# Accumulating transfers for some low weight parts, five more Strassen-like units, and another order of shared additions in a split-precision encoder trunk

## The chip, the cores and the metric

One core of a Trainium2 chip. The metric is device time in microseconds (us) from the first to the last instruction of one execution and what lies around it; a run's number is the time of that one core, and the number given for a kernel is the median of its runs.

## The reference, cut to what matters

256 tokens of width D = 2048 pass two layers (a 2-D neighbourhood attention, then a short gated convolution). Each mixer is followed by a gated MLP with a width-3 convolution and D_FF = 5632. All is float32.

```python
def conv_glu_ffn(x, w_up, conv_w, conv_b, w_down):
    h = dwconv_centered(x @ w_up, conv_w) + conv_b
    g, u = jnp.split(h, 2, axis=-1)
    return (jax.nn.silu(g) * u) @ w_down

for i in range(DEPTH):                      # DEPTH = 2
    a = rms_norm(h, mix_norm[i])
    mixed = neighborhood_attention(...) if i == 0 else short_conv_mixer(...)
    h = h + mixed                           # both end in "@ w_o" / "@ w_out", 2048 x 2048
    h = h + conv_glu_ffn(rms_norm(h, ffn_norm[i]), ...)
return rms_norm(h, final_norm)
```

The change is in the products that return to the width of 2048: attention's output (`wo`), the short convolution's output (`wscout`) and the MLP's down projection (`wdown`), which each add to `h`.

## The kernel before

**Split products.** A float32 operand is written as a high part `hi` (rounded to the type that TensorE takes at full rate) and a low part `lo` = value minus `hi`. `product` (L355 to L359) makes a product from three matmuls into one PSUM bank: L357 activation-high x weight-high, L358 activation-high x weight-low, L359 activation-low x weight-high.

**Weights.** A chunk of 512 KB (128 x 1024) is loaded on SP's queue into a buffer `raw` (L109 in row layout, L113 in the column layout of the groups below). `parts` (L119) then splits it: ScalarE casts it to `hi` (L128), VectorE subtracts to make `lo` (L129). There are 5 `raw`, 6 `hi` and 6 `lo` buffers, and `prep_to` (L101) runs four chunks (AHEAD) ahead of TensorE. A chunk's `raw` comes free when its last reader is done, and SP's next load waits for that.

**Phases** (`Phase`, L144) do the up projections, qkv and the input of the short convolution; TensorE's rows of it are L174 and L182. **Groups** (`Tokens`, L292) do the projections that return to 2048 columns. An MLP is done in two halves of 22 tiles of 128 hidden channels; after each half a `Tokens` adds its share to `h`. A `Tokens` has two column groups g = 0, 1 of 1024 columns; four PSUM banks ("mm": 11, 21, 12, 22, two token halves by two column halves) collect a group's sums. The group's depth goes by units of two tiles, unit i being tiles 2i and 2i+1, and each unit has a left and a right chunk.

- A *normal* unit does eight products (24 matmuls of 128x512): the left chunk's four, then the right chunk's four.
- A unit in the set `sset` is a *seven* (L361): seven products of combined operands. Its right chunk goes through `sums` (L132), four VectorE additions of 128x512 (L138 to L141) that make two combined weight tiles, one of them in another `raw` buffer; three splits follow (a half-size w22, and t13 and t24). The combined activations ("forms") come from `make_forms` (L396): four POOL operations and a split of 128x512. Four products go to banks of their own, a, e, f, b ("mu", in the buffers that other stages use under the tags st, sc, tr, o), which stay open from the group's first seven to its last. In the order in which they run, the seven products write a, 11, 12, e, f, b, 21.

At a group's end four residual additions (L262, VectorE) add the mm banks to `h` and so free them for the next group. After the last seven, `combine` (L380) copies a (L384, ScalarE) and adds e, f, b to `h` with eight VectorE operations; the line `after(due, ...)` in `seven` queues it for so many ticks later, a tick being one item of TensorE's work, so `due` says behind which residuals and low parts it stands.

**Plans.** For each `Tokens` a table gives, per group, the units' order, the sevens and `due`: `S_FIRST` for the first half of an MLP, `S_SECOND` for the second, `S_ATT` for attention's output, `S_OUT` for the short convolution's. Groups start in the profile at 308.4 us (`wo`), 644.7, 1003.8, 1390.6 (`wscout`), 1723.1 and 2082.1 and end 57 to 118 us later.

The order on each engine is the program's own order after a scheduling layer has moved instructions; each engine runs its queue in order and waits for semaphores.

Of the kernel before, what the change touches and what calls it, by code (L numbers as in the profile page):

```python
# [16 lines left out]
F32R = mybir.dt.float32r  # L17
AF = mybir.ActivationFunctionType
ALU = mybir.AluOpType
# [3 lines left out]
P = 128  # L23
D = 2048
S = 256
KT = D // P
# [8 lines left out]
CH = 8  # L35
# [4 lines left out]

ORDER = tuple(range(HALF // 2))
S_FIRST = ((ORDER, (1, 3, 5, 7, 9), 3), (ORDER, (3, 5, 7, 9), 6))

S_SECOND = (((0, 2, 1, 4, 3, 6, 5, 8, 7, 9, 10), (1, 3, 5, 7), 1), (ORDER, (3, 5, 7), 1))
S_OUT = (1, 3, 5)
S_ATT = (((0, 1, 2, 6, 3, 7, 4, 5), (6, 7), 1),) * 2


C_NORM = 0
# [9 lines left out]
def trunk(ctx, tc, xT, par, bias, wqk, wv, wo, wsc, wscout, wup, wdown, out):  # L61
    nc = tc.nc
# [41 lines left out]
    def prep_to(n):  # L104
        while len(prepped) < min(n, len(chunks)):
            src, w, kind = chunks[len(prepped)]
            raw = wp.tile([P, CH * P], F32, name="raw", tag="raw", bufs=5)
            if kind == "rows":
                nc.sync.dma_start(out=raw[:, :w], in_=src)  # L109
                prepped.append(parts(raw[:, :w]) + (raw,))  # L110
                continue

            nc.sync.dma_start(out=raw.rearrange("p (f c) -> p f c", f=4), in_=src.rearrange("f p c -> p f c"))  # L113
            r = raw.rearrange("p (f k c) -> p f k c", f=4, c=P)
            if kind == "cols":
                prepped.append(parts(r) + (raw,))
            else:
                prepped.append(sums(prepped[-1][2].rearrange("p (f k c) -> p f k c", f=4, c=P), r))

    def parts(r):  # L120

        hi = wp.tile([P, CH * P], F32R, name="hi", tag="hi", bufs=6)
        lo = wp.tile([P, CH * P], F32R, name="lo", tag="lo", bufs=6)
        if len(r.shape) == 4:
            hv, lv = (x[:, :4 * r.shape[2] * P].rearrange("p (k f c) -> p f k c", f=4, c=P) for x in (hi, lo))
        else:
            hv, lv = (x[:, :r.shape[1]] for x in (hi, lo))
        nc.scalar.copy(out=hv, in_=r)  # L128
        nc.vector.tensor_sub(out=lv, in0=r, in1=hv.bitcast(F32))  # L129
        return hi, lo  # L130

    def sums(l, r):  # L132

# [158 lines left out]
    class Tokens:  # L292
# [4 lines left out]
        def __init__(self, w, nk, src, evac, plan, forms, halves=0):  # L297


            self.src, self.evac, self.plan, self.forms, self.nk = src, evac, plan, forms, nk  # L300
            self.halves = halves
            for g, (order, sset, _) in enumerate(plan):
                for i in order:
                    k = 2 * i
                    left, right = (w[f:f + 4, :, k * P:(k + 2) * P] for f in (8 * g, 8 * g + 4))
                    c = len(chunks)
                    if g == KT // 8 - 1 and k >= nk - halves:
                        if k == nk - halves:
                            items.append((self, g, c, k, k, nk))
                            ends.append(c + halves)  # L310
                        chunks.extend(((left, 8 * P, "cols"), (right, 8 * P, "cols")))
                        continue
                    chunks.append((left, 8 * P, "cols"))
                    if i in sset:
                        chunks.append((right, 8 * P, "sums"))
                        items.append((self, g, c + 1, k, k, k + 2))
                        ends.append(c + 2)
                    else:
                        chunks.append((right, 8 * P, "cols"))
                        items.append((self, g, c, k, k, k + 2))  # L320
                        items.append((self, g, c + 1, k, k, k + 2))
                        ends.extend((c + 1, c + 2))

        def run(self, g, c, k0, ka, kb):
            order, sset, _ = self.plan[g]
            if kb - ka > 2:
                return self.finale(g, c, ka)
            if k0 // 2 in sset:
                return self.seven(g, c, k0)
            hi, lo, _ = prepped[c]  # L330
            right = len(prepped[c - 1]) == 3 and (self, g, c - 1, k0, ka, kb) in items[item[0] - 1:item[0]]
            first, last = ka == 2 * order[0], kb == 2 * order[-1] + 2
            if first and not right:
                self.c = {n: pm.tile([P, 4 * P], F32, name="mm", tag="mm") for n in ("11", "21", "12", "22")}
            for t in range(2):
                ps = self.c["12"[t] + "12"[right]]
                for k in range(ka, kb):
                    x = self.src[k]
                    wh, wl = (w[:, (k - k0) * 4 * P:(k - k0 + 1) * 4 * P] for w in (hi, lo))
# [20 lines left out]

        def seven(self, g, c, k0):  # L361
            i = k0 // 2
            order, sset, due = self.plan[g]
            s_order = [j for j in order if j in sset]
            first, last = i == s_order[0], i == s_order[-1]
            if first:
                self.u = [pa.tile([P, 4 * P], F32, name="mu", tag=n) for n in ("st", "sc", "tr", "o")]
            a, e, f, b = self.u
            left, (w22, t13, t24) = prepped[c - 1], prepped[c]
            fh, fl = self.forms[i]  # L370
            s1, s2, s4, s3 = ((fh[:, j * P:(j + 1) * P], fl[:, j * P:(j + 1) * P]) for j in range(4))
            raw = lambda k, t: tuple(self.src[k0 + k][:, j + t * P:j + (t + 1) * P] for j in (0, S))
            for ps, x, w, j in ((a, raw(0, 0), left, 0), (self.c["11"], raw(1, 0), left, 1), (self.c["12"], s4, w22, 0),
                                (e, s1, t13, 0), (f, s3, t13, 1), (b, s2, t24, 0), (self.c["21"], raw(1, 1), t24, 1)):
                own = ps in self.u
                self.product(ps, *x, *(y[:, j * 4 * P:(j + 1) * 4 * P] for y in w[:2]), own and first, own and last)
            if last:
                after(0 if self.halves and g == KT // 8 - 1 else due, lambda u=self.u: self.combine(g, *u))

        def combine(self, g, a, e, f, b):  # L380

            sa, u = (tp.tile([P, 4 * P], F32, name="s", tag="s") for _ in range(2))
            o = {(t, n): h[:, t, (2 * g + n) * 4 * P:(2 * g + n + 1) * 4 * P] for t in range(2) for n in range(2)}
            nc.scalar.copy(out=sa, in_=a)  # L384
            nc.vector.tensor_add(out=u, in0=b, in1=sa)
# [328 lines left out]
    Tokens(wscout, KT, yT, to_norm(3, a3), ((range(KT // 2), S_OUT, 1),) * 2, yforms)  # L714
    mlp(1, a3, last_evac())


# [132 lines left out]
```

## Time and profile before

| | |
|---|---|
| median of 3 runs | 2214.65 us (2214.26 to 2214.70) |
| the profiled execution | 2215.03 us, of which the span is 2213.2 us |
| granted TensorE clock, mean | 0.998 |
| TensorE (PE) busy | 2198.8 us, 99% of the span |
| VectorE (DVE), ScalarE (ACT), GpSimd (POOL) busy | 1743.6, 1275.6, 71.5 us |
| DMA engines, mean busy share | 58.2% for SP's weight loads |

In the profile's lines the columns are: busy time, mean nanoseconds of one, and the idle time of the engine just before, with what ended most of it ("<- DVE lo L129": a semaphore from that line). In a timeline the columns are the start and length in us, then engine, line, operation, output and inputs, and in brackets the idle time before. PE's instructions are pipelined: one that takes 0.39 us starts 0.23 us after the last. "DMA to landing" or the third column of the DMA issues is the time from a DMA's issue until its bytes have landed. PEld is TensorE's weight load, which runs beside its matmuls.

### The profile page before, as it was taken

The numbers are of one execution on the slowest core, as the hardware profiler recorded it, in microseconds if no ns is written. First come the engines' busy times: TensorE is split into PE (matmuls) and PEld (weight loads), VectorE is DVE, ScalarE is ACT, GpSimd is POOL, SyncE is SP. The second block draws the span as 40 slices with busy tenths as digits, with TensorE's granted clock in tenths as the row PEclk, the third lists the DMA queues.
The fourth block names the chain that finished last, engine by engine and source line by source line (L and its number), as shares of the span: only waits on it lengthen the run. The fifth ranks groups of instructions, "written<-read, shape, count | busy, mean of one in ns | idle before, by whom it ended". The sixth has DMA issues, their size and how long they took to land.

```text
span 2213.2 us, 31934 instructions
## 1 busy us (share of the span) xinstructions
PE 2198.8 (99%) x11782; PEld 1902.3 (86%) x11782; DVE 1743.6 (79%) x2665; ACT 1275.6 (58%) x1896; POOL 71.5 (3%) x115
## 2 busy tenths in 40 slices
PE   9999999999999999999999999999999999999998
PEld 8888888888888888888888888888888888888886
DVE  8677678877788877778876666888777888777887
ACT  7555556666655566665654445566566555666554
POOL 0100010000000000000000000000000000000000
PEclk9999999999999999999999999999999999999999
DMA  7565546555556755555655555565555566555564
GB/s 253 187 201 173 177 147 214 192 191 190 191 171 200 226 185 195 187 188 182 201 195 189 190 189 187 172 219 182 193 188 181 171 211 216 191 190 191 171 200 133
DMA packets 214605, 421.00 MB, mean 190 GB/s; under 512 B 13488, under 2 KB 142640, under 8 KB 214448
## 3 DMA queue, kind: packets, MB, share of 16 engines
q1 hardware_dynamic: 213072, 418.33, 58.2%
q8 instruction: 92, 1.51, 0.3%
q10 hardware_dynamic: 1376, 0.63, 0.1%
q14 instruction: 65, 0.53, 0.1%
HBM read 416.81 MB, written 2.10 MB: 189 GB/s over the span
## 4 chain that ended last, share of the span: by engine, by line
PE 94%; DVE 2%; DMA 2%; ACT 1%; issue 1%; SPq 0%; DVEq 0%; ACTq 0%
PE mm L174 40%; PE mm L182 21%; PE mm L357 7%; PE mm L359 7%; PE mm L358 7%; PE mu L358 2%; PE mu L359 2%; PE mu L357 2%; PE mm L547 1%; PE mm L545 1%; PE mm L546 1%; DMA raw<-in_wdown 1%; DVE lo L129 1%; PE tr L273 1%; DMA raw<-in_wqk 1%
## 5 line engine op out<-in xcount | busy, mean ns | idle before, releaser
L129 DVE TENSOR_TENSOR lo<-raw,hi 128x1024 fp32r<-128x1024 f32 (+1 forms) x834 | 971.5, 1187 | 190.7 <-PE mm L182 123.8
L128 ACT CAST hi<-raw 128x1024 fp32r<-128x1024 f32 (+1 forms) x834 | 847.5, 1021 | 374.2 <-PE mm L359 112.4
L174 PE MATMUL mm<-a,hi 128*128 128x512 f32 x4096 | 962.3, 391 | 0.3 <-DVE a L215 0.3
L174 PEld LDWEIGHTS mm<-a,hi 128*128 128x128 f32 x4096 | 759.5, 188 | 153.0 <-DVE a L215 1.6
L182 PEld LDWEIGHTS mm<-a,lo 128*128 128x128 f32 x4096 | 512.9, 191 | 12.0
L182 PE MATMUL mm<-a,lo 128*128 128x256 f32 x4096 | 518.1, 283 | 0.0
L357 PE MATMUL mm<-hi,act 128*128 128x512 f32 x708 | 276.9, 391 | 0.0
L359 PE MATMUL mm<-hi,act 128*128 128x512 f32 x708 | 276.2, 390 | 0.0
L358 PE MATMUL mm<-lo,act 128*128 128x512 f32 x708 | 275.8, 390 | 0.1
L227 ACT COPY corr<-mm 128x256 f32<-128x256 f32 x256 | 95.3, 373 | 242.2 <-PE mm L182 242.2
L243 DVE SCALAR_TENSOR_TENSOR conv<-pad,pt,conv 128x256 f32<-128x256 f32 x384 | 185.1, 483 | 44.3 <-ACT conv L241 29.3
L241 ACT ACTIVATE conv<-pad,pt 128x256 f32<-128x256 f32 x176 | 106.1, 604 | 145.4 <-DVE pad L233 145.4
L359 PEld LDWEIGHTS mm<-hi,act 128*128 128x128 f32 x708 | 132.9, 188 | 28.4
L358 PEld LDWEIGHTS mm<-lo,act 128*128 128x128 f32 x708 | 133.0, 188 | 28.2 <-DVE lo L129 0.5
L357 PEld LDWEIGHTS mm<-hi,act 128*128 128x128 f32 x708 | 132.9, 188 | 27.7 <-DVE h L262 0.3
L207 DVE TENSOR_TENSOR act<-conv,act 128x256 fp32r<-128x256 f32 x88 | 38.0, 432 | 89.5 <-ACT act L206 89.5
L228 DVE TENSOR_TENSOR corr<-mm,corr 128x256 f32<-128x256 f32 x256 | 107.1, 419 | 0.2 <-ACT corr L227 0.2
L233 DVE TENSOR_TENSOR pad<-corr,rstd 128x256 f32<-128x256 f32 x176 | 74.2, 423 | 0.1
L138 DVE TENSOR_TENSOR raw<-raw 128x512 f32<-128x512 f32 x42 | 29.0, 691 | 50.6 <-DMA raw<-in_wdown 47.3
L128 ACT CAST hi<-t 128x1024 fp32r<-128x1024 f32 x42 | 44.2, 1052 | 40.7 <-DVE t L141 31.3
L129 DVE TENSOR_TENSOR lo<-t,hi 128x1024 fp32r<-128x1024 f32 x42 | 51.3, 1222 | 3.2 <-ACT hi L128 2.8
L545 PE MATMUL mm<-hi,a 128*128 128x512 f32 x128 | 50.3, 393 | 0.0
(157 smaller groups left out, 1448.8 us busy)
## 6 DMA issues: line engine op xcount, KB each, us to landing
raw<-in_wup SPq DMA_DIRECT2D x352, 512.0 KB, 5.0
raw<-in_wdown SPq DMA_DIRECT2D x176, 512.0 KB, 4.7
raw<-in_wsc SPq DMA_DIRECT2D x96, 512.0 KB, 5.1
raw<-in_wqk SPq DMA_DIRECT2D x56, 512.0 KB, 4.6
raw<-in_wv SPq DMA_DIRECT2D x32, 512.0 KB, 4.5
raw<-in_wo SPq DMA_DIRECT2D x32, 512.0 KB, 4.5
raw<-in_wscout SPq DMA_DIRECT2D x32, 512.0 KB, 4.5
raw<-in_wqk SPq DMA_DIRECT2D x16, 256.0 KB, 5.2
```

The costliest lines, as they stand in the source:

```text
L128: nc.scalar.copy(out=hv, in_=r)
L129: nc.vector.tensor_sub(out=lv, in0=r, in1=hv.bitcast(F32))
L174: nc.tensor.matmul(self.ps[ft], lhsT=prepped[i][0][:, o:o + P], rhs=self.src[k], start=k == 0, stop=False)
L182: nc.tensor.matmul(self.ps[ft][:, S:], lhsT=prepped[i][1][:, o:o + P], rhs=self.src[k][:, :S], start=False, stop=k == self.nk - 1)
L227: nc.scalar.copy(out=corr, in_=ps[:, S:])
L228: nc.vector.tensor_add(out=corr, in0=ps[:, :S], in1=corr)
L233: nc.vector.tensor_mul(out=dst, in0=both(ps), in1=rstd)
L241: nc.scalar.activation(c, x[:, 1:S + 1], AF.Identity, scale=w[1], bias=b)
L243: nc.vector.scalar_tensor_tensor(out=c, in0=x[:, tap:tap + S], scalar=w[tap], in1=c, op0=ALU.mult, op1=ALU.add)
L357: nc.tensor.matmul(ps, lhsT=xh, rhs=wh, start=start, stop=False)
L358: nc.tensor.matmul(ps, lhsT=xh, rhs=wl, start=False, stop=False)
L359: nc.tensor.matmul(ps, lhsT=xl, rhs=wh, start=False, stop=stop)
```

## The change

Three things, all within `Tokens` and `prep_to`.

**A third kind of chunk.** The plans get a fourth field, the units whose right chunk is `added`: 2, 4, 6, 8 in both groups of `S_FIRST` and group 0 of `S_SECOND`, 2, 4, 6 in its group 1, 1, 2 and 2, 3 in `S_ATT`, 2, 4 in both groups of `wscout`. With two layers of MLP these are 38 chunks. For such a chunk ScalarE writes minus the high part into `lo` (a copy with scale -1), a DMA of GpSimd's queue adds `raw` to it from SBUF to SBUF, and ScalarE casts `hi` as before; VectorE's subtraction of 128 x 1024 is gone. PE's second matmul of the chunk now waits for that DMA, and so does SP's load that takes the same `raw` buffer next.

**Five more sevens.** Unit 1 in group 1 of `S_FIRST` and unit 9 in group 0 of `S_SECOND` (each in two layers), and unit 5 in group 0 of `S_ATT`. TensorE has 15 matmuls less. The order of group 0 of `S_SECOND` is now natural, its `due` 0 instead of 1; group 0 of `S_ATT` goes 0, 5, 1, 6, 2, 7, 3, 4. Units 9 (`S_SECOND`, two layers) and 5 (`S_ATT`) had no form until now.

**combine's order.** Same operations; the sum f + u and the addition to o[1, 0] stand earlier.

```diff
-S_FIRST = ((ORDER, (1, 3, 5, 7, 9), 3), (ORDER, (3, 5, 7, 9), 6))
+S_FIRST = ((ORDER, (1, 3, 5, 7, 9), 3, (2, 4, 6, 8)), (ORDER, (1, 3, 5, 7, 9), 6, (2, 4, 6, 8)))
...
-S_ATT = (((0, 1, 2, 6, 3, 7, 4, 5), (6, 7), 1),) * 2
+S_ATT = (((0, 5, 1, 6, 2, 7, 3, 4), (5, 6, 7), 1, (1, 2)), ((0, 1, 2, 6, 3, 7, 4, 5), (6, 7), 1, (2, 3)))
...
+            elif kind == "added":
+                prepped.append(added_parts(raw, r) + (raw,))
...
+    def added_parts(raw, r):
+
+        hi = wp.tile([P, CH * P], F32R, name="hi", tag="hi", bufs=6)
+        lo = wp.tile([P, CH * P], F32R, name="lo", tag="lo", bufs=6)
+        nc.scalar.activation(lo, raw, AF.Copy, scale=-1.0)
+        nc.gpsimd.dma_start(out=lo, in_=raw, accum_op=ALU.add)
+        nc.scalar.copy(out=hi.rearrange("p (k f c) -> p f k c", f=4, c=P), in_=r)
+        return hi, lo.rearrange("p (f k c) -> p f k c", f=4, c=P)
...
-                        chunks.append((right, 8 * P, "cols"))
+                        chunks.append((right, 8 * P, "added" if i in added else "cols"))
...
             nc.vector.tensor_sub(out=sa, in0=e, in1=u)
+            nc.vector.tensor_add(out=u, in0=f, in1=u)
             nc.vector.tensor_sub(out=o[1, 1], in0=o[1, 1], in1=f)
-            nc.vector.tensor_add(out=u, in0=f, in1=u)
+            nc.vector.tensor_add(out=o[1, 0], in0=o[1, 0], in1=u)
             nc.vector.tensor_add(out=o[0, 1], in0=o[0, 1], in1=sa)
             nc.vector.tensor_add(out=o[1, 1], in0=o[1, 1], in1=sa)
-            nc.vector.tensor_add(out=o[1, 0], in0=o[1, 0], in1=u)
```

The lines of the code move by 3 to 13: L128 and L129 become L131 and L132, the sums L150 to L153, the products' L357 to L359 L370 to L372, the residual L262 L274, combine's L384 to L392 L397 to L405.

On ScalarE, in the steady state of group 0 of the first half in layer 0, a period of one seven and one normal unit was, before (`128x4x2x128` is a whole chunk in column layout, `t_...` the tile t24, `128x512` the half-size w22):

```order
L128 CAST hi<-raw 128x4x2x128 x3
L128 CAST hi<-raw 128x512
L128 CAST hi<-raw 128x1024
L128 CAST hi<-t_10716 128x1024
L128 CAST hi<-raw 128x4x2x128 x3
```

and is now:

```order
L131 CAST hi<-raw 128x4x2x128
L139 ACTIVATE lo<-raw 128x1024
L141 CAST hi<-raw 128x4x2x128
L131 CAST hi<-raw 128x4x2x128
L131 CAST hi<-raw 128x512
L131 CAST hi<-raw 128x1024
L131 CAST hi<-t_10266 128x1024
L131 CAST hi<-raw 128x4x2x128
```

The negation (L139) stands between the normal unit's left cast and its right cast; nothing else changes place there.

On VectorE, at the boundary between the two groups of the first half in layer 0, before (L262 residuals, L385 to L392 combine, L129 low parts):

```order
L262 TENSOR_TENSOR h<-mm,h 128x512
L387 TENSOR_TENSOR s<-mu,s 128x512
L262 TENSOR_TENSOR h<-mm,h 128x512
L129 TENSOR_TENSOR lo<-raw,hi 128x4x2x128 x2
L388 TENSOR_TENSOR h<-h,mu 128x512
L389 TENSOR_TENSOR s<-mu,s 128x512
L390 TENSOR_TENSOR h<-h,s 128x512
```

and now, from the operation ahead of the fourth residual to combine's fifth, the last reader of bank f (L402):

```order
L400 TENSOR_TENSOR s<-mu,s 128x512
L274 TENSOR_TENSOR h<-mm,h 128x512
L150 TENSOR_TENSOR raw<-raw 128x512
L151 TENSOR_TENSOR raw<-raw 128x512
L152 TENSOR_TENSOR t_7097<-raw 128x512
L132 TENSOR_TENSOR lo<-raw,hi 128x512
L153 TENSOR_TENSOR t_7097<-t_7097,raw 128x512
L132 TENSOR_TENSOR lo<-raw,hi 128x1024
L401 TENSOR_TENSOR s<-mu,s 128x512
L132 TENSOR_TENSOR lo<-t_7097,hi 128x1024
L132 TENSOR_TENSOR lo<-raw,hi 128x4x2x128
L402 TENSOR_TENSOR h<-h,mu 128x512
```

The four sums and three splits of unit 1, which was normal, stand now between the last residual and the operations that read f, and the low part of unit 2's left chunk behind them.

On VectorE at the same boundary of the second half, before (the two low parts ahead are of chunks of the next group):

```order
L129 TENSOR_TENSOR lo<-raw,hi 128x4x2x128 x3
L385 TENSOR_TENSOR s<-mu,s 128x512
L388 TENSOR_TENSOR h<-h,mu 128x512
L387 TENSOR_TENSOR s<-mu,s 128x512
L129 TENSOR_TENSOR lo<-raw,hi 128x4x2x128
L389 TENSOR_TENSOR s<-mu,s 128x512
L390 TENSOR_TENSOR h<-h,s 128x512
L391 TENSOR_TENSOR h<-h,s 128x512
L392 TENSOR_TENSOR h<-h,s 128x512
L262 TENSOR_TENSOR h<-mm,h 128x512 x2
```

and now:

```order
L132 TENSOR_TENSOR lo<-raw,hi 128x4x2x128 x2
L398 TENSOR_TENSOR s<-mu,s 128x512
L400 TENSOR_TENSOR s<-mu,s 128x512
L274 TENSOR_TENSOR h<-mm,h 128x512
L401 TENSOR_TENSOR s<-mu,s 128x512
L402 TENSOR_TENSOR h<-h,mu 128x512
L403 TENSOR_TENSOR h<-h,s 128x512
L404 TENSOR_TENSOR h<-h,s 128x512
L405 TENSOR_TENSOR h<-h,s 128x512
L274 TENSOR_TENSOR h<-mm,h 128x512
```

The combine is one seven later in the group than before and one tick less is waited, so that its operations run between the first and the second residual; in layer 1 one more low part stands between L398 and L400.

More of the change, by code (lines that the diff above doesn't have):

```diff
@@ L43 @@
 ORDER = tuple(range(HALF // 2))
[L44 to L46 removed]
+S_FIRST = ((ORDER, (1, 3, 5, 7, 9), 3, (2, 4, 6, 8)), (ORDER, (1, 3, 5, 7, 9), 6, (2, 4, 6, 8)))
+S_SECOND = ((ORDER, (1, 3, 5, 7, 9), 0, (2, 4, 6, 8)), (ORDER, (3, 5, 7), 1, (2, 4, 6)))
 S_OUT = (1, 3, 5)
[L48 removed]
+S_ATT = (((0, 5, 1, 6, 2, 7, 3, 4), (5, 6, 7), 1, (1, 2)), ((0, 1, 2, 6, 3, 7, 4, 5), (6, 7), 1, (2, 3)))
 C_NORM = 0
@@ L301, in __init__ @@
             self.halves = halves
-            for g, (order, sset, _) in enumerate(plan):
+            for g, (order, sset, _, added) in enumerate(plan):
                 for i in order:
@@ L324, in run @@
         def run(self, g, c, k0, ka, kb):
-            order, sset, _ = self.plan[g]
+            order, sset = self.plan[g][:2]
             if kb - ka > 2:
@@ L338, in run @@
                     x = self.src[k]
-                    wh, wl = (w[:, (k - k0) * 4 * P:(k - k0 + 1) * 4 * P] for w in (hi, lo))
+                    wh = hi[:, (k - k0) * 4 * P:(k - k0 + 1) * 4 * P]
+                    wl = lo[:, :, k - k0, :] if len(lo.shape) == 4 else lo[:, (k - k0) * 4 * P:(k - k0 + 1) * 4 * P]
                     xh, xl = (x[:, i + t * P:i + (t + 1) * P] for i in (0, S))
@@ L362, in seven @@
             i = k0 // 2
-            order, sset, due = self.plan[g]
+            order, sset, due, _ = self.plan[g]
             s_order = [j for j in order if j in sset]
@@ L713, in trunk @@
     Phase(wsc, range(3 * KT), KT, a2, sc_evac, intro=3)
-    Tokens(wscout, KT, yT, to_norm(3, a3), ((range(KT // 2), S_OUT, 1),) * 2, yforms)
+    Tokens(wscout, KT, yT, to_norm(3, a3), ((range(KT // 2), S_OUT, 1, (2, 4)),) * 2, yforms)
     mlp(1, a3, last_evac())
```

## Prediction

> **What bounds the kernel now.** I read the page first, then TensorE's waits, then the windows of the stages that change, then the timelines of one stage.
>
> ```profile
> span 2213.2 us, 31934 instructions
> PE 2198.8 (99%) x11782; PEld 1902.3 (86%) x11782; DVE 1743.6 (79%) x2665; ACT 1275.6 (58%) x1896; POOL 71.5 (3%) x115
> PE 94%; DVE 2%; DMA 2%; ACT 1%; issue 1%; SPq 0%; DVEq 0%; ACTq 0%
> ```
>
> PE is busy for 99% of the span and makes up 94% of the chain that ended last. What it waits for in the whole run:
>
> ```profile
> engine line waited for: us in total, times, longest us
> PE sc L475 <- DVE s L482: 2.4, 1, 2.4
> PE bc L661 <- DVE conv L659: 1.6, 1, 1.6
> PE tr L500 <- DVE act L207: 1.2, 1, 1.2
> PE st L89 <- DVE inv L620: 1.1, 1, 1.1
> PE tr L644 <- DVE h L262: 0.8, 1, 0.8
> PE mm L174 <- DVE a L215: 0.3, 1, 0.3
> ```
>
> That is 7.4 us, and no row is of the down groups' products (L357 to L359). So a microsecond taken off VectorE or ScalarE there is worth nothing by itself; only removed PE work shortens the run, and only a new PE wait lengthens it. The stage of the first half's down groups in layer 0:
>
> ```profile
> core 0: us, PE busy (x) PEld busy (x) DVE busy (x) ACT busy (x) POOL busy (x), PEclk, DMA share, GB/s
> 644.70:759.30 114.60, 114.60 (x504) 94.12 (x503) 98.85 (x120) 63.07 (x68) 0.00 (x0) 1.00 0.67 206
> ```
>
> PE fills its 114.6 us at full granted clock. DVE has 99 of them, ACT 63, POOL none, the DMA engines two thirds.
>
> **The five units.** One period of the steady state is a seven and a normal unit:
>
> ```profile
> 670.78 0.39 PE L357 MATMUL mu<-hi,act 128*128 128x512 f32 x1
> 675.63 0.40 PE L357 MATMUL mm<-hi,act 128*128 128x512 f32 x1
> ...
> 678.37 0.39 PE L357 MATMUL mm<-hi,act 128*128 128x512 f32 x1
> 678.60 0.39 PE L358 MATMUL mm<-lo,act 128*128 128x512 f32 x1
> ...
> 681.09 0.39 PE L357 MATMUL mu<-hi,act 128*128 128x512 f32 x1
> ```
>
> The seven starts at 670.78, the normal unit's left half at 675.63, its right half at 678.37, the next seven at 681.09. A seven takes 4.85 us, a normal unit 5.46, a period 10.31. Five units turned into sevens remove 5 x 0.61 = 3.0 us. The upper bound is 15 matmuls at the spacing of 0.23 us between 678.37 and 678.60: 3.4 us.
>
> Each new seven also costs DVE four additions and two more low parts in two halves, and ACT two casts more; three of the five units need a form they did not have, four POOL operations each. DVE's share is weighed below where it can reach PE; POOL and ACT do theirs in the idle time of the window row.
>
> **The 38 added transfers.** Each takes one DVE subtraction away and puts an ACT negation, a POOL DMA and PE's wait for it in its place:
>
> ```profile
> 671.02 1.05 ACT L128 CAST hi<-raw 128x1024 fp32r<-128x1024 f32 x1 [1.47 <-PE mm L359]
> ```
> ```profile
> 674.12 0.68 DVE L139 TENSOR_TENSOR raw<-raw 128x512 f32<-128x512 f32 x1
> 674.72 0.69 DVE L140 TENSOR_TENSOR t<-raw 128x512 f32<-128x512 f32 x1
> 675.32 1.22 DVE L129 TENSOR_TENSOR lo<-raw,hi 128x1024 fp32r<-128x1024 f32 x1
> 676.46 0.69 DVE L141 TENSOR_TENSOR t<-t,raw 128x512 f32<-128x512 f32 x1
> ```
>
> On DVE a subtraction of 128x1024 occupies 1.14 us from start to start, an addition of 128x512 0.60. The ACT row is the cast of the right chunk that PE needs at 678.37; it could not start before PE had let go of its buffer. I take the negation at the same 1.05 us, from the same moment, so it ends at 672.1. PE's first use of the low part is at 678.60, which leaves the transfer T 6.5 us before PE waits. (That PE waits delays all behind it, since its queue is in order.)
>
> T is not in the trace. The nearest rows:
>
> ```profile
> raw<-in_wdown SPq DMA_DIRECT2D x176, 512.0 KB, 4.7
> out<-a SPq DMA_DIRECT2D x12, 128.0 KB, 2.0
> ```
>
> Below, 2.0 us, a quarter of the bytes. Above, 9.4 us, twice a weight load, since an accumulation reads two tiles of 512 KB. I take 4.7, the row with the same bytes written: then the low part lands at 676.8, near where DVE's now ends (676.5), and PE does not wait: 0 us.
>
> There is a second condition. There are five raw buffers, and a period uses five, so an added chunk's buffer serves the next added chunk. Load, negation and transfer must turn round in one period: 4.7 + 1.05 + T against 10.31, so each turn is late by T - 4.56. At T = 4.7 that is 0.14, which the spare 6.5 - 4.7 = 1.8 us absorbs over a group's four added chunks. SP's load of the buffer now waits for the transfer, and the loads behind it in SP's queue wait too; at 4.7 they start where they do now. The 38 subtractions (38 x 1.14 = 43 us of DVE) go from an engine that PE does not wait for: 0 us. The 38 negations (40 us) fall on ACT, which is idle 45% of such a stage: 0 us, and if its cover were gone each would be a microsecond of delay inside the same 1.8.
>
> The Trainium skill's page "DMA: Bandwidth & Descriptors", section on the anatomy of one DMA on the SWDGE path, gives 2.0 us plus bytes over 436 GB/s, so 3.2 us for such a transfer as an estimate; no run here shows it yet, and by it the sum is unchanged.
>
> **The boundary of the first half's groups.** Here the trace says more. Group 0's last seven ends and its last unit starts at 696.26; group 1 starts at 701.72:
>
> ```profile
> 696.26 0.40 PE L357 MATMUL mm<-hi,act 128*128 128x512 f32 x1
> ...
> 701.72 0.39 PE L357 MATMUL mm<-hi,act 128*128 128x512 f32 x1
> ```
> ```profile
> 697.75 1.23 DVE L129 TENSOR_TENSOR lo<-raw,hi 128x1024 fp32r<-128x1024 f32 x1 [0.25 <-ACT hi L128]
> 698.90 0.68 DVE L385 TENSOR_TENSOR s<-mu,s 128x512 f32<-128x512 f32 x1
> ...
> 703.75 0.68 DVE L262 TENSOR_TENSOR h<-mm,h 128x512 f32<-128x512 f32 x1
> ```
> ```profile
> 695.20 1.05 ACT L128 CAST hi<-raw 128x1024 fp32r<-128x1024 f32 x1 [1.66 <-DMA raw<-in_wdown]
> ```
>
> DVE's low parts wait there for ACT's casts, those for loads, and the fourth residual (L262) ends at 704.43, 2.7 us after the group starts. Today nobody minds, because group 1's first seven is unit 3. Now it is unit 1, at 5.46 us. Its fifth product starts the bank f anew, so PE needs f free at 5.46 + 4 x 0.69 = 8.2 us. The last reader of f is combine's fifth DVE operation, and the changed order puts between the fourth residual and its end: six additions of 128x512 or the like with one small low part (6 x 0.60), three low parts of 128x1024 (3 x 1.14), and itself (0.69), 7.7 us in all. With the residual at 2.7 that ends at 10.4, and PE waits 2.2 us. The residual cannot end before 0.9 (PE's last product of group 0 plus 0.7), and then PE waits 0.4. In the changed kernel unit 8's low part is off DVE, so the loads behind it can be issued about 1.1 us earlier and the whole row moves up by that or more; I take 0.8 us per layer, in the middle of that movement: 2 x 0.8 = 1.6 us.
>
> **The boundary of the second half's groups.** The combine of group 0 now stands in front of the residuals (due 0 in place of 1). Group 1's second bank is needed six matmuls of 0.227 us, 1.36 us, into the group, 6.8 us after the last seven's end. From the combine's first DVE operation to the end of the second residual are nine operations of 0.6, 5.5 us; layer 1 has one low part more among them, 6.6. If the combine starts as late as L385 does above (2.64 us after 696.26), the waits are 1.3 and 2.5; a load wait as at 695.20 once more on top, 1.7, gives 3.0 and 4.2. If it starts when the seven ends, 0 and 0. With it 0.9 after, between the two for the same reason as above: 0 and 0.7. I take 0.7.
>
> The order of sums inside combine frees no bank earlier or later (f's last reader is the fifth before and after): 0 us. In the attention output, form 5 keeps a buffer that a cast of the last heads' scores would use; that cast comes after the scores it then waits for, so 0, with 1 us above for the range.
>
> **Sum.** -3.0 + 0 + 1.6 + 0.7 = -0.7 us. The profiled execution took 2215.03 us (span 2213.2 and 1.8 around it), which gives 2214.3; it stands 0.4 above the median of the runs, 2214.65, so on their scale **2213.9 us**. A measurement of this kernel tells some 0.2%, 4.4 us, from no change, and the forecast is inside.
>
> **Rivals.**
>
> *A: the transfer is late, and slower is the outcome.* T decides. Once the spare 6.5 - T is used up, each further turn in a group delays PE by T - 4.56; with four added chunks (three turns) that begins at T = 5.0. At 5.9, a load and one DVE subtraction's length: 3 x 1.34 - 0.6 = 3.4 us in each of six groups of four, 2.1 in two of three, 0.7 in four of two, together 27.6, so 2213.9 + 27.6 = 2241.5. At 5.3 the same sum is 6 x 1.0 + 2 x 0.3 = 6.6, so 2220.5. For it: the queue is new, the accumulation reads two tiles, the DMA engines are already 0.67 busy in the stage. Against it: turns shorten when loads are less crowded. This is also what a page's rule would do: DVE has two-input work without pause, and if it kept POOL from writing descriptors, T would grow by the rest of a DVE instruction, up to 1.2 us, to the 5.9 above. The Trainium skill's "SBUF — State Buffer", section on who interferes with whom, says that a DVE instruction with two SBUF inputs contends with GpSimd work that reads SBUF, and the same page that a software-queue DMA starves in DVE's two-port modes; the traces of before hold no DMA of POOL's queue, so none bears it out. I give 5.0 to 5.5 a chance of 0.12 and over that 0.18. The upper end of T, 9.4, would be over 150 us worse; it is left out of the range.
>
> *B: the boundaries stall at their upper ends.* 2 x 2.2 + 3.0 + 4.2 and 1 for attention, less 3.0, is +9.6 against the profiled time: 2224.2 on the runs' scale. For it: loads landed late at 695.20. Against: low parts that were ahead of them are gone. Chance 0.12, of which half is within 0.2%.
>
> *C: nothing stalls.* -3.4 at the most: 2211.3, still within 0.2%. More would need PE to lose work that is not removed: PE's waits outside (7.4 us) are elsewhere. Chance 0.15; faster by over 0.2% 0.04 in addition.
>
> *D: the change does not do what it says,* for example the scheduler moves a transfer behind its use. The order shows each transfer ahead of its use on the queues; chance 0.02, in A's.
>
> **Numbers.** Forecast 0.39, C 0.15, half of B 0.06, and A's mild end 0.06 are within 0.2%: 0.66. Slower: 0.06 of B, 0.06 of A's mild end, 0.18 of A: 0.30. Faster 0.04. The range goes from C with a little under it, 2211.0, to B's end at 2224.0; outside are A's strong end (0.18) and little else. The likeliest case alone spans 2211.3 to 2218.
>
> **What would show it.** PE's rows fall by 15, and the stage at 644.7 is shorter by 0.6 plus what its boundary waits. If T is 4.7, POOL's DMA row lo<-raw shows about that from issue to landing, and PE's table of waits has no row for a DMA of lo. If A holds, that table has such a row with the microseconds, and the waits grow within each group from the second added unit to the last. If the boundary terms hold, there are one row for bank f (mu waiting for h of L402) of about 0.8 us twice and one for mm waiting for the residual, L274, and nothing else near 700 and 1058. The forecast is wrong if the DMA wait exceeds 5 us in all, or if PE's work itself does not fall by 3 us.

## The result and the profile after

The changed kernel takes 2240.78 us (median of 4 runs, 2240.58 to 2241.83) against 2214.68 for the kernel before beside it: 1.012 times as long, 95% interval 1.0108 to 1.0131. The forecast was 2213.9, no change, with a range to 2224. The price of rival A at a transfer of 5.9 us, 2241.5, is near the result. Of all executions timed for this document one, of the last kernel in the table of experiments, took 4626.61 us, about twice the others; it counts in that kernel's median and not in its ratio.

The page of the changed kernel, the lines that answer to those of before, with the new transfer's queue and its time from issue to landing:

```profile
span 2239.1 us, 32083 instructions
PE 2202.8 (98%) x11767; PEld 1897.8 (85%) x11767; DVE 1724.0 (77%) x2660; ACT 1315.1 (59%) x1948; POOL 113.0 (5%) x165
...
q0 software_dynamic: 5472, 19.93, 4.6%
...
raw<-in_wdown SPq DMA_DIRECT2D x176, 512.0 KB, 4.9
lo<-raw POOLq DMA_DIRECT2D x38, 512.0 KB, 5.5
```

PE has 15 instructions less, and its idle time (span less busy time) is 36.3 us where it was 14.4. The transfers take 5.5 us in the median, and 4.6% of 16 engines' span is 103 us of all engines, 2.7 us for each transfer. The weight loads became slower, 4.9 for 4.7. What PE waits for:

```profile
engine line waited for: us in total, times, longest us
PE mm L371 <- DMA lo<-raw: 17.0, 16, 2.9
...
PE tr L657 <- DVE h L274: 2.3, 2, 1.5
PE mm L370 <- DVE h L274: 1.8, 2, 1.1
...
PE mu L370 <- ACT s L534: 1.0, 1, 1.0
...
PE mu L370 <- DVE h L402: 0.3, 1, 0.3
```

The first row is new: the second matmul of an added chunk waits for its transfer. Counted from start to start against the usual 0.23 us, the waits at L371 are 20 us. (Some expectations below say 24; that figure comes out when three places are counted too where PE did other work, or waited for VectorE, between two matmuls of a product.)

By stages, from the first to the last product of each, before and after: attention's output 88.9 and 90.8; first half, layer 0: 114.4 and 119.9; second half 117.3 and 120.7; short convolution's output 85.4 and 87.0; layer 1's halves 114.4 and 122.9, 119.9 and 124.5. That is 25.4 of the 25.9 us by which the span grew; everything between these stages kept its time within 0.5.

Where it comes from in a group is seen in the first half of layer 0. ScalarE in its first group (L139 is the negation):

```profile
662.27 1.06 ACT L139 ACTIVATE lo<-raw 128x1024 fp32r<-128x1024 f32 x1 [1.40 <-PE mm L371]
...
673.97 1.06 ACT L139 ACTIVATE lo<-raw 128x1024 fp32r<-128x1024 f32 x1 [2.77 <-DMA raw<-in_wdown]
```
```profile
663.63 0.86 POOL L140 DMA_DIRECT2D lo<-raw  x1 [9.44 <-ACT lo L139]
675.32 0.86 POOL L140 DMA_DIRECT2D lo<-raw  x1 [10.83 <-ACT lo L139]
686.15 0.86 POOL L140 DMA_DIRECT2D lo<-raw  x1 [9.97 <-ACT lo L139]
```
```profile
669.52 0.37 SPq L114 DMA_DIRECT2D raw<-in_wdown  x1
```

The turn of the raw buffer that the prediction described is there: the transfer issued at 663.63 lands at 669.33, the load waits for it and is issued at 669.52, and the next negation, which until then had waited for PE, now waits 2.77 us for that load. The turns are 11.7 and 10.8 us long against the period of 10.3. Yet in this group PE waits only 0.7 us for transfers. In the second group it waits 3.9, and there the first transfer begins late. ScalarE there:

```profile
707.79 1.05 ACT L131 CAST hi<-raw 128x1024 fp32r<-128x1024 f32 x1 [5.49 <-DVE raw L151]
...
711.50 1.04 ACT L141 CAST hi<-raw 128x1024 fp32r<-128x1024 f32 x1
712.45 1.06 ACT L139 ACTIVATE lo<-raw 128x1024 fp32r<-128x1024 f32 x1
```

and PE, where unit 2's right chunk begins:

```profile
718.12 0.39 PE L370 MATMUL mm<-hi,act 128*128 128x512 f32 x1
719.89 0.50 PE L371 MATMUL mm<-lo,act 128*128 128x512 f32 x1 [1.38 <-DMA lo<-raw]
```

The new seven's sums stand on VectorE behind the residuals, ScalarE's casts wait 5.5 us for them, and the first negation of the group starts 5.9 us ahead of PE's need at 718.35. From there 1.06 us of negation, 0.3 until the issue and 6.0 of transfer follow, and it lands at 719.84.

### The profile page after: what moved, and what is told of

It reads as the page before. It is cut to its first block, busy times and chain, and to the rows that moved or that the text cites. A ratio compares the mean times of both kernels' runs of the same rounds, so it can differ in the third digit from the quotient of the medians.

```text
span 2239.1 us, 32083 instructions
## 1 busy us (share of the span) xinstructions
PE 2202.8 (98%) x11767; PEld 1897.8 (85%) x11767; DVE 1724.0 (77%) x2660; ACT 1315.1 (59%) x1948; POOL 113.0 (5%) x165
## 3 DMA queue, kind: packets, MB, share of 16 engines
q0 software_dynamic: 5472, 19.93, 4.6%
## 5 line engine op out<-in xcount | busy, mean ns | idle before, releaser
L132 DVE TENSOR_TENSOR lo<-raw,hi 128x1024 fp32r<-128x1024 f32 (+1 forms) x801 | 930.7, 1182 | 213.3 <-PE mm L194 119.0
L131 ACT CAST hi<-raw 128x1024 fp32r<-128x1024 f32 (+1 forms) x801 | 809.1, 1015 | 331.2 <-PE mm L186 97.8
L371 PE MATMUL mm<-lo,act 128*128 128x512 f32 x678 | 266.4, 393 | 17.2 <-DMA lo<-raw 17.0
L370 PE MATMUL mm<-hi,act 128*128 128x512 f32 x678 | 265.8, 392 | 1.8 <-DVE h L274 1.8
L372 PE MATMUL mm<-hi,act 128*128 128x512 f32 x678 | 264.6, 390 | 0.0
L371 PEld LDWEIGHTS mm<-lo,act 128*128 128x128 f32 x678 | 127.3, 188 | 51.2 <-DMA lo<-raw 25.0
L370 PEld LDWEIGHTS mm<-hi,act 128*128 128x128 f32 x678 | 127.3, 188 | 29.4 <-DVE h L274 2.7
L372 PEld LDWEIGHTS mm<-hi,act 128*128 128x128 f32 x678 | 127.3, 188 | 26.8
L150 DVE TENSOR_TENSOR raw<-raw 128x512 f32<-128x512 f32 x47 | 32.5, 691 | 77.3 <-DMA raw<-in_wdown 66.0
L139 ACT ACTIVATE lo<-raw 128x1024 fp32r<-128x1024 f32 x38 | 40.2, 1059 | 47.8 <-DMA raw<-in_wdown 21.9
L140 POOL DMA_DIRECT2D lo<-raw x38 | 32.9, 866 | 625.2 <-ACT lo L139 536.3
L131 ACT CAST hi<-t 128x1024 fp32r<-128x1024 f32 x47 | 49.3, 1049 | 24.0 <-DVE t L153 17.1
```

The lines of the kernel that those rows point to most:

```text
L370: nc.tensor.matmul(ps, lhsT=xh, rhs=wh, start=start, stop=False)
L371: nc.tensor.matmul(ps, lhsT=xh, rhs=wl, start=False, stop=False)
L372: nc.tensor.matmul(ps, lhsT=xl, rhs=wh, start=False, stop=stop)
```

## The experiments

The kernels and what they took; "MLP stages" is the sum of the four down stages in the profile, from first to last product, "wait" what PE's table of waits has for lo<-raw, "T" the transfer's median from issue to landing. The last three columns are of one execution each, which can lie off the median: the profiled one of "transfers only" took 2219.43 us, of "VectorE adds" 2217.26, of "traffic alone" 2223.40.

| kernel | us | ratio, 95% interval | MLP stages, us | wait, us | T, us |
|---|---|---|---|---|---|
| before | 2214.65 | | 466.0 | | |
| changed | 2240.78 | 1.0108 to 1.0131 | 487.9 | 17.0 | 5.5 |
| changed, once more | 2240.71 | 1.0102 to 1.0132 | 486.6 | 14.8 | 5.4 |
| sevens only | 2216.19 | 0.9999 to 1.0018 | 466.9 | | |
| transfers only | 2223.10 | 1.0019 to 1.0045 | 469.8 | 1.7 | 5.5 |
| VectorE adds | 2215.03 | 0.9992 to 1.0011 | 467.7 | | |
| every second | 2229.52 | 1.0051 to 1.0081 | 478.5 | 9.6 | 6.5 |
| plain copy | 2224.14 | 1.0032 to 1.0059 | 474.6 | 4.4 | 4.3 |
| unit 1 normal | 2225.27 | 1.0039 to 1.0070 | 472.8 | 5.4 | 5.3 |
| three sevens, other due | 2216.48 | 1.0000 to 1.0017 | 467.0 | | |
| traffic alone | 2226.77 | 1.0041 to 1.0068 | 474.4 | | |
| from unit 4 | 2237.62 | 1.0092 to 1.0122 | 485.1 | 12.5 | 5.5 |
| GpSimd negates two | 2240.33 | 1.0106 to 1.0140 | 486.9 | 14.1 | 5.4 |
| GpSimd does both | 2238.88 | 1.0098 to 1.0128 | 475.7 | | |
| GpSimd adds | 2217.55 | 1.0006 to 1.0026 | 463.9 | | |
| GpSimd adds, MLP only | 2213.30 | 0.9988 to 1.0006 | 463.9 | | |

The theory was that the transfer is too long for its place and PE waits for it; the rivals, that the sevens and boundaries, or ScalarE's load, cost the time.

**Sevens only.**

```diff
-                        chunks.append((right, 8 * P, "added" if i in added else "cols"))
+                        chunks.append((right, 8 * P, "cols"))
```

> The changed kernel with every added chunk made as a normal one again (VectorE's subtraction, no accumulating transfer); the five sevens and the new orders stay. Theory T (the transfer is too long for its place, PE waits for it): the waits of PE for lo<-raw, 24 us of start-to-start excess in the changed kernel, are gone, the other new waits (two boundaries and attention, 4 us) stay, the sevens save 3: 2240.8 - 24 - about 1 = 2215 to 2217 us. Rival S (the sevens and the boundaries cost the time, the transfers only carry the wait): stays above 2228.

2216.19 us: without transfers 24.6 of the 26 us are gone.

**Transfers only.** Old orders, sevens and dues, with the fourth field.

```diff
-S_FIRST = ((ORDER, (1, 3, 5, 7, 9), 3, (2, 4, 6, 8)), (ORDER, (1, 3, 5, 7, 9), 6, (2, 4, 6, 8)))
+S_FIRST = ((ORDER, (1, 3, 5, 7, 9), 3, (2, 4, 6, 8)), (ORDER, (3, 5, 7, 9), 6, (2, 4, 6, 8)))
-S_SECOND = ((ORDER, (1, 3, 5, 7, 9), 0, (2, 4, 6, 8)), (ORDER, (3, 5, 7), 1, (2, 4, 6)))
+S_SECOND = (((0, 2, 1, 4, 3, 6, 5, 8, 7, 9, 10), (1, 3, 5, 7), 1, (2, 4, 6, 8)), (ORDER, (3, 5, 7), 1, (2, 4, 6)))
-S_ATT = (((0, 5, 1, 6, 2, 7, 3, 4), (5, 6, 7), 1, (1, 2)), ((0, 1, 2, 6, 3, 7, 4, 5), (6, 7), 1, (2, 3)))
+S_ATT = (((0, 1, 2, 6, 3, 7, 4, 5), (6, 7), 1, (2, 3)), ((0, 1, 2, 6, 3, 7, 4, 5), (6, 7), 1, (2, 3)))
```

> The kernel before with the 38 added transfers alone: its plans, sevens and dues, with the fourth field set as in the change (attention's group 0: 2 and 3); the order of combine's additions is the new one. Theory T: 2214.7 + 24 to 28 = 2239 to 2243 us. Rival S: under 2225.

2223.1 us, under the rival's 2225, though the run before had come out at theory T's number. T is 5.5 as in the changed kernel, but PE's table of waits has

```profile
PE mm L371 <- DMA lo<-raw: 1.7, 3, 1.1
```

So T alone does not set the loss. (Its profiled execution was the fastest of five and shows 4.4 of the 8.5 us.) Sevens cost 1.5, transfers 8.5, both together 26: the two meet somewhere.

**VectorE adds.**

```diff
-        nc.gpsimd.dma_start(out=lo, in_=raw, accum_op=ALU.add)
+        nc.vector.tensor_add(out=lo, in0=raw, in1=lo.bitcast(F32))
```

> The changed kernel with ScalarE's negation kept, but VectorE adds raw to it (128x1024, in place) where the transfer stood. All the load on ScalarE stays, the transfer and its traffic go. Theory T: 2215 to 2218 us. Rival A (ScalarE's 38 extra negations of 1.06 us in its in-order queue push the casts back): stays above 2228.

2215.03 us: ScalarE's 38 negations cost nothing that can be measured.

**Every second.** The others likewise: (2, 6) in the second half, one unit per group in the two short stages.

```diff
-S_FIRST = ((ORDER, (1, 3, 5, 7, 9), 3, (2, 4, 6, 8)), (ORDER, (1, 3, 5, 7, 9), 6, (2, 4, 6, 8)))
+S_FIRST = ((ORDER, (1, 3, 5, 7, 9), 3, (2, 6)), (ORDER, (1, 3, 5, 7, 9), 6, (2, 6)))
```

> The changed kernel with added chunks only in every second normal unit: 2 and 6 of each down group, one in each group of attention's output and the short convolution's, 20 transfers in place of 38. Theory T in the form of the prediction's rival (the loss is the turn of one raw buffer, which an added chunk hands to the next added chunk one period later; with a period between there is no lateness to hand on): PE waits under 4 us in all, 2215 to 2220 us. Rival C (each transfer costs alike, by its traffic or its own length): 20/38 of 24 us, 12.6, so 2228 us.

2229.52 us, near the rival's number, and PE waits 9.6 us for transfers where the theory had under 4. The form "only the turn from one added chunk to the next" has fallen. But the transfers were longer here, 6.5 us in the median: by the trace's packets the first of them follows the issue by 2.4 us in the median, up to 3.8, where the changed kernel has 1.75, with loads ahead of it. Why they met more loads at this spacing I did not find out.

**Plain copy.**

```diff
-        nc.gpsimd.dma_start(out=lo, in_=raw, accum_op=ALU.add)
+        nc.gpsimd.dma_start(out=lo, in_=raw)
```

> The changed kernel with the transfer as a plain copy of raw into lo, without the accumulation: same queue, same waits, same 512 KB written. What is computed is changed: the low part of the 38 chunks is then the whole weight. In the changed kernel a transfer shows at the median 1.75 us from issue to its first packet (1.43 at least), 2.7 us of all 16 DMA engines, and 0.3 to the landing. Theory T (the double reading makes it too long): the packets take about the 1.47 us at which weight loads follow one another, T falls to 3.2 to 4.0, PE's waits for lo nearly go: 2215 to 2220 us. Rival Q (the queue and the chain of waits cost the time, whatever the bytes): T stays over 4.7 and the time over 2230.

2224.14 us: 16.6 less than the changed kernel, and between the two expectations. PE waits 4.4 us for the copies. That the transfer accumulates, in place of copying, is thus most of the loss: by the packets, a copy keeps 16 engines busy for 1.44 us in the median, an accumulation for 2.7. The page's queue row says the same:

```profile
q0 software_dynamic: 5472, 19.93, 2.6%
```

2.6% against 4.6%. The row counts the same 19.93 MB for both, so a second reading is not seen there as bytes, only as time.

**Unit 1 normal.**

```diff
-S_FIRST = (..., (ORDER, (1, 3, 5, 7, 9), 6, (2, 4, 6, 8)))
+S_FIRST = (..., (ORDER, (3, 5, 7, 9), 6, (2, 4, 6, 8)))
```

> The changed kernel with unit 1 of the first half's second group normal again; all 38 added transfers and the other three sevens stay. Theory L (lead: with a seven right behind the boundary the first added chunk of the group is issued 4.5 us ahead of its use in place of some 10, and from there each turn adds its lateness): those groups' waits, 4.5 and 6.2 us for lo and 0.6 for bank f, go, two savings of 0.6 go too: 2230 to 2232 us. Rival N (each transfer costs what it costs wherever it stands): 2239 to 2242.

2225.27 us: 15.5 less, more than theory L expected. This one seven, in two layers, is where sevens and transfers meet. ScalarE and GpSimd at the same place as above:

```profile
705.05 1.05 ACT L141 CAST hi<-raw 128x1024 fp32r<-128x1024 f32 x1 [0.45 <-DVE lo L132]
706.00 1.06 ACT L139 ACTIVATE lo<-raw 128x1024 fp32r<-128x1024 f32 x1
```
```profile
707.35 0.86 POOL L140 DMA_DIRECT2D lo<-raw  x1 [20.62 <-PE mm L372]
```

The transfer is issued at 707.35 for a first use at 718.04, 10.7 us ahead, in place of 713.80 for 718.35, 4.5 ahead.

**From unit 4.**

```diff
-S_FIRST = (..., (ORDER, (1, 3, 5, 7, 9), 6, (2, 4, 6, 8)))
+S_FIRST = (..., (ORDER, (1, 3, 5, 7, 9), 6, (4, 6, 8)))
```

> The changed kernel with unit 2's right chunk a normal one in the second group of the first half (two layers); the seven at unit 1 and 36 transfers stay. In the changed kernel that chunk's negation waits in ScalarE's queue behind a cast of unit 1's combined weights, which waits 5.5 us for VectorE's sums, and those stand behind the residuals; it starts at 712.45 though raw has landed at 706.03. Theory Q (that first late chunk hands its lateness on from turn to turn): the two groups' waits for lo, 3.9 and 6.2 us, nearly go, and what the loads lose by them: 2226 to 2232 us. Rival U (the seven at unit 1 makes the buffers tight for all later chunks too): over 2236.

2237.62 us: rival U. The first transfer of the group, now unit 4's, is issued at 726.66 and lands at 732.48, 2.5 us late. The lateness is not handed on by the first chunk alone; what the boundary put back still stands on ScalarE one period later: its cast that waits for the sums of unit 3 starts at 720.65, in "unit 1 normal" at 714.50, while the group starts only 1.5 us later (705.68 and 704.22).

**GpSimd negates two.** For unit 2 of that group alone:

```diff
-        nc.scalar.activation(lo, raw, AF.Copy, scale=-1.0)
+        nc.gpsimd.tensor_scalar(out=lo, in0=raw, scalar1=-1.0, scalar2=None, op0=ALU.mult)
```

> The changed kernel with the negation of that one chunk per layer (unit 2, second group, first half) on GpSimd in place of ScalarE; all 38 transfers and sevens stay. GpSimd is idle there; a negation of 128x1024 by it should take 3 to 4 us (its 128x384 takes 1.33). Theory Q (ScalarE's queue in order is what makes it late): it ends near 710 in place of 713.5, the transfer lands near 716, ahead of its use at 718.2, and the groups' waits fall by half or more: 2228 to 2236 us. Rival R (raw, lo or the DMA engines are late anyway): no gain, 2239 to 2243, more if GpSimd is slower than thought.

2240.33 us, no gain: rival R. GpSimd could not begin at 706 either:

```profile
709.91 3.25 POOL L140 TENSOR_SCALAR lo<-raw 128x1024 fp32r<-128x1024 f32 x1 [22.97 <-PE mm L374]
```

It waits for PE to let go of a `lo` buffer. A seven takes four of the six, a normal unit two. So ScalarE's queue is not the only reason; behind it stands the buffer. GpSimd's negation is also three times as long, so the transfer is issued at 713.45, hardly ahead of the 713.80 of the changed kernel, and what an earlier one would have been worth this run does not tell. The changed kernel itself once more, on the same chip:

> The changed kernel itself once more, beside the other two on the same chip, as their measure: 2240 to 2242 us by its first timing.

It took 2240.71 us (2237.06 to 2242.61). Its profile has 122.4, 118.4, 123.0 and 122.8 us for the four MLP stages, where the first one has 119.9, 120.7, 122.9 and 124.5: a single stage moves by up to 2.5 us from one execution to the next, their sum here by 1.3.

**Traffic alone.** As "VectorE adds", and after the cast of `hi`:

```diff
+        for s in spare:
+            nc.gpsimd.dma_start(out=s, in_=hi.bitcast(F32))
```

with two tensors of 128x1024 in HBM as `spare`.

> As the run in which VectorE adds in place of the transfer, and beside each of the 38 chunks two plain transfers of 512 KB on GpSimd's queue from hi to a spare tensor in HBM, which nothing reads: about as much time of the 16 DMA engines as one accumulating transfer (two of 1.47 us against 2.7), but nobody waits for their end. Theory D (the DMA engines' time: loads stand behind the transfer and come late): at least half of the loss, over 2227 us. Theory W (PE and the raw buffer wait for the transfer's own end; the loads have room): 2214 to 2220.

2226.77 us, 11.7 over "VectorE adds" (its profiled execution 6.1 over), at the edge of theory D's number: bytes on the same DMA engines that nobody waits for cost nearly half of the loss by the medians, a quarter by the profiles. The loads grew from 4.5 to 4.9 us in the median. The share of these transfers, 5.3%, is a little over the accumulations' 4.6%, and they write to HBM, so it is not quite the same load.

**GpSimd does both, GpSimd adds.** A path without any transfer: the negation on GpSimd as above, for all 38, and the addition, or the addition alone.

```diff
-        nc.gpsimd.dma_start(out=lo, in_=raw, accum_op=ALU.add)
+        nc.gpsimd.tensor_add(out=lo, in0=raw, in1=lo.bitcast(F32))
```

> The changed kernel with negation and addition of the 38 chunks both on GpSimd (128x1024 each; the negation took 3.25 us there, the addition should take 3.3 to 4, so the path is 6.6 to 7.5 us long, as with the transfer), and no transfer. ScalarE's negations go. Theory P (the length of the chunk's path against its lead): 2228 to 2240 us, with PE's waits for lo in the second group of the first half as in the changed kernel. Theory D (the DMA engines' time): 2214 to 2219, since no bytes move.

> The changed kernel with ScalarE's negation kept and the addition on GpSimd (128x1024) in place of the transfer: a path of 1.1 + 0.3 + 3.3 to 4 = 4.7 to 5.4 us, without transfer. Theory P: between, as with the plain copy, whose path was 5.7: 2215 to 2222. Theory D: 2214 to 2218. More than 2225 would mean that GpSimd and VectorE slow each other.

The first took 2238.88 us, which looks like theory P, but not by theory P's waits. Its path is 6.1 us long in the median, against 6.8 with the transfer, and yet the profile shows nobody waiting for GpSimd's addition. PE waits for VectorE, whose instructions grew beside GpSimd's:

```profile
1056.99 2.66 POOL L140 TENSOR_TENSOR lo<-raw,lo 128x1024 fp32r<-128x1024 f32 x1
...
1057.31 3.42 DVE L132 TENSOR_TENSOR lo<-raw,hi 128x1024 fp32r<-128x1024 f32 x1
...
1060.78 0.50 PE L371 MATMUL mm<-lo,act 128*128 128x512 f32 x1 [1.42 <-DVE lo L132]
```

That low part takes 1.22 us elsewhere. So the 475.7 - 467.7 = 8 us that the MLP stages cost over "VectorE adds", and the 15.9 us that the two short stages lost (88.9 to 100.2 and 85.4 to 90.0), are no price of the path's length, and theory P stays untested. The second took 2217.55 us; its path is 3.6 us, and in its MLP stages PE waits for nothing that the table shows. They take 463.9 us, 2.1 less than before the change, which is nearly what four sevens save.

**The rest.** Could the sevens pay at all? With sevens where nothing seemed to wait, and every fourth field empty:

```diff
+S_FIRST = ((ORDER, (1, 3, 5, 7, 9), 3, ()), (ORDER, (3, 5, 7, 9), 6, ()))
+S_SECOND = ((ORDER, (1, 3, 5, 7, 9), 2, ()), (ORDER, (3, 5, 7), 1, ()))
+S_ATT = (((0, 1, 5, 2, 6, 3, 7, 4), (5, 6, 7), 1, ()), ((0, 1, 2, 6, 3, 7, 4, 5), (6, 7), 1, ()))
```

> No added transfers; sevens beyond the kernel before only where nothing waits for them: unit 9 of the second half's first group (two layers) with due 2, so that its combine stands behind the residuals, and unit 5 of attention's first group, at the third place of the order (0, 1, 5, 2, 6, 3, 7, 4) so that the banks are free. By PE's work 3 x 0.61 = 1.8 us less than before: 2212.9 us. If the boundaries cost as much as in the run with sevens alone: 2215 to 2216.

2216.48 us: no. The combine behind the residuals brought waits at the same boundary, 2.1 us in two places for its first addition to `h` (L399). And "GpSimd adds" with the two short stages as before:

```diff
+S_ATT = (((0, 1, 2, 6, 3, 7, 4, 5), (6, 7), 1, ()),) * 2
+    Tokens(wscout, KT, yT, to_norm(3, a3), ((range(KT // 2), S_OUT, 1, ()),) * 2, yforms)
```

> The MLP's down groups as in the run with GpSimd's addition (30 chunks, four new sevens), attention's output and the short convolution's as in the kernel before (no added chunks, no new seven). If the stages keep their times: 88.9 + 463.8 + 85.4 = 638.1 us against 640.3 before, 2.2 less, so 2212 to 2213 us. If the gain there came from the late start of the stages behind attention: 2214 to 2216.

2213.30 us, the same as before within the interval (0.9988 to 1.0006). The profile shows the saving, 638.1 us in the six stages against 640.3:

```profile
span 2210.4 us, 32028 instructions
```

but the runs do not separate it from no change.

## Why the prediction was wrong

**The step that failed** is the one that took T = 4.7 and from it "PE does not wait: 0 us". The measured transfer takes 5.5 us in the median (4.5 to 8.0), is issued 0.3 us after the negation's end, which the step left out, and PE waits 20 us for it. The row that was taken, a weight load's 4.7, is near the shortest transfers only: the six in "transfers only" during which no load lands took 4.7 to 5.7, four of them 4.7 to 4.8. The prediction had both ends (2.0 and 9.4) and the reason for more, that two tiles are read; it gave that reason to the upper end and not to the middle. By the packets a transfer is at the least 1.4 us to the first packet, then 2.7 us of all 16 engines, and 0.3 to the landing. The same step took one lead, 6.5 us from the negation's end, for all units; it was read in the steady state, and behind the new seven it does not hold: there 4.8 us are left (713.51 to 718.35).

**A term is missing.** The DMA engines' own time does not stand in the sum; their "0.67 busy" stands only among the arguments for rival A. In the same stage they are now (columns as in the prediction's row of that stage):

```profile
646.50:766.90 120.40, 116.45 (x502) 93.31 (x501) 93.70 (x116) 71.36 (x78) 6.90 (x8) 1.00 0.79 230
```

0.79 in the mean. Before, loads around a boundary already followed one another every 1.47 us (landings at 695.10, 696.57 and 698.04); each transfer takes 2.7 us of the same engines. "Traffic alone" shows that such traffic costs some 6 to 12 us by itself.

**The boundary** was priced as a wait for bank f, 0.8 us twice; that wait was 0.5 in layer 0 (0.3 in the table) and did not show in layer 1; in the second profile of the changed kernel it was 0.6 and 0.9. It was about right and beside the point: the same seven uses up the lead in which the transfer should have run, and that is worth 15.5 us ("unit 1 normal"). The prediction added the two edits as separate terms; measured apart they are +1.5 and +8.5, together +26. The second half's boundary was 0.9 and 1.2 where 0 and 0.7 were taken; the other bound, attention's 1 us, came in full, in another form (PE waits for a bank that ScalarE still reads, L534).

**The sevens** save what was said: start to start, a seven in the changed kernel still takes 4.85 us (651.99 to 656.84 in the trace). The ACT term of 0 was right ("VectorE adds", 2215.03). The DVE term of 0 that run does not test, since VectorE still adds there. Where VectorE is free of the work and no transfer runs ("GpSimd adds"), the MLP stages take 463.9 us against 466.9 with "sevens only": by single profiles, relief of VectorE was worth some 3 us, in waits of PE that "sevens only" has (1.1 us for L274, 0.8 for L402, 0.6 for low parts) and "GpSimd adds" does not.

**Rival A** had the right sign and by its sum nearly the right size: with the measured 5.5 and the 0.3 ahead of it, T = 5.8, it gives 23.8 us, so 2237.7. But that nearness is in good part luck, for its mechanism is only part of it. It gave 3.4 us to each group of four, while the trace has 0.7 and 1.9 in the first half's first groups, 3.9 and 6.2 in its second groups, 2.5 and 2.3 in the second half's first groups and none in its second ones (in the second profile 2.3 and 1.0, 4.3 and 4.6, 0.5 and 2.1, none). Nor do the waits grow within a group, as its sign said: in layer 0's second group they are 1.5, 0.6, 1.6 and 0.3. Nor is T = 5.0 the point from which it decides: "transfers only" has the same 5.5 and loses a third.

The estimate of 3.2 us from the Trainium skill's "DMA: Bandwidth & Descriptors", section on the anatomy of one DMA on the SWDGE path, falls short of the measured 5.5, and of a plain copy's 4.3 (3.3 at the least). Of the rule in the Trainium skill's "SBUF — State Buffer", section on who interferes with whom, that a software-queue DMA starves while VectorE is in its two-port modes, these runs show no clear sign, and none was made to test it: GpSimd's issue took 0.86 us nearly throughout, the first packet followed 1.43 us after its start at the least, and while the longest transfer ran three loads landed.

**What stays open:** how the two parts, the chunk's long path and the traffic, add up. In the MLP stages of the profiles the traffic alone costs 7 us and both cost 20; no run prices the path alone. That `lo` buffers are short behind the boundary is read from one wait; no run had more of them. And the loss at every second unit, where fewer transfers took longer each, is only told, not explained.

## What to carry to other kernels

A transfer that replaces an engine's instruction is priced by three numbers, its own length with the transfers it will meet, the DMA engines' time that it takes from the loads, and the shortest lead that any of its users has; the mean idle share of an engine or of the DMA engines answers none of them. Here an accumulating transfer took 1.8 to 1.9 times the engine time of a copy of the same bytes (4.6% and 2.6% in the queue rows, 2.7 and 1.44 us by the packets). Two edits that use the same slack must be priced together, above all at a boundary between groups, where the lead is shortest.

## What else the runs showed of the hardware

After a wait of 2.3 us PE ran slower for a while, in "from unit 4" (the clock granted between 732.6 and 737 us was 0.61):

```profile
732.52 0.50 PE L371 MATMUL mm<-lo,act 128*128 128x512 f32 x1 [2.31 <-DMA lo<-raw]
...
734.00 0.63 PE L371 MATMUL mm<-lo,act 128*128 128x512 f32 x1
734.43 0.63 PE L372 MATMUL mm<-hi,act 128*128 128x512 f32 x1
...
736.97 0.40 PE L372 MATMUL mu<-hi,act 128*128 128x512 f32 x1
```

Some eight matmuls start 0.43 us apart in place of 0.23, 1.6 us more. In the kept profiles PE waits 2 us or longer 23 times; after 14 of these waits such slow matmuls follow and after 9 they do not. In the changed kernel's own profile they follow one of 2.5 us and not one of 2.9. What decides is not known here.

GpSimd's addition of 128x1024 with two inputs in SBUF took 2.4 us where VectorE stood idle, and VectorE's additions beside it grew: L150's mean in "GpSimd adds" is 1191 ns, 691 in the changed kernel.

```profile
L150 DVE TENSOR_TENSOR raw<-raw 128x512 f32<-128x512 f32 x47 | 56.0, 1191 | 37.9 <-DMA raw<-in_wdown 29.4 <-DMA raw<-in_wo 5.2 <-DMA raw<-in_wscout 3.3
```

This agrees with the Trainium skill's "SBUF — State Buffer", section on who interferes with whom: a VectorE instruction with two SBUF inputs contends with GpSimd work that reads SBUF.
